# Read-back of the first products of a SwiGLU layer, moved behind one-element copies, with its stores on GpSimd's queue

## The chip, the cores and the metric

The kernel runs on one core of a Trainium2 chip. The metric is device time in microseconds (us): the median of the runs of one program. PE is TensorE's matmuls, PEld its weight loads, DVE is VectorE, ACT is ScalarE, POOL is GpSimd, and SPq is the queue of the sync engine, which issues most of the DMAs. L1422 is line 1422 of the kernel.

## The reference

One step of an encoder layer for two groups of tokens that share weights: 1024 prompt tokens and 64 sample tokens, 1088 together, 1024 channels, fp32. The layer has stick-breaking attention beside an mLSTM, a merge by gates and an output projection; then the feed-forward part, which is where the change lies:

```python
u2 = _rmsnorm(x, norm2_g) * (1 + sc2) + sh2
x = x + g2 * ((jax.nn.silu(u2 @ w_ff_gate) * (u2 @ w_ff_up)) @ w_ff_down)
```

`w_ff_gate` and `w_ff_up` are 1024 by 2816, `w_ff_down` is 2816 by 1024. At the end comes one more RMSNorm.

## The kernel before, in words

Matmuls run in fp32r with each operand split in a high and a low part, three matmuls for one product. Gate, up and down products use a Strassen-like scheme with seven products for eight (numbered p, in the order 1, 6, 5, 7, 2, 3, 4), over sums and differences of weight blocks and of quarters of the tokens.

The 2816 feed-forward channels are 22 blocks of 128. One run of `gate_up(i, h, ...)` makes block i for half h of the tokens (544 of them): seven products of 12 matmuls, each evacuated from PSUM by `evac(p)`. At p = 6 VectorE writes the tile `u2`, which the later products of the same run read (the tag has one buffer). The product tile `hst`, two quarters of 272 tokens, is stored to `h_d` in memory by the sync queue at L1375.

The jobs are, in order: blocks 0 to 9 for half 0 alone (job k = 0 to 9, `NF` is 10); blocks 10 to 21 for both halves (jobs 10 to 21); blocks 0 to 9 for half 1. For blocks 0 to 9 the weight sums come ready-made from memory (`wsum_d`), seven loads a job by L1310. From block 10 on the raw gate and up weights are loaded (L1298), and GpSimd makes the sums S (L1324, L1325, L1331, L1334). ScalarE casts a weight to its high part (L47), VectorE makes the low part by a difference (L56). The raw weights have three buffers and one smaller one, the split weights seven, one for each product.

The down product reads `h_d` and, in `tb_d` and `tc_d`, sums and differences of the products of neighbouring blocks. For most of them `pair_sums` makes these on VectorE when the products are there (L1404 to L1414). For half 0 of blocks 0 to 9 they are made by `first_sums`, a generator with five steps j: it loads the products of blocks 2j and 2j + 1 from `h_d` into the two halves of the one tile `tj` (L1422, L1423), and at its next call makes four sums on GpSimd (L1425 to L1428) and stores both halves (L1429, L1430). It is called at p = 6 in each half of jobs 10 to 21, ten calls in all: `step(early_sums)` in `hook`. While jobs 0 to 9 run, `todo` makes the modulated input of the second half, on VectorE and ScalarE.

The program text is not the order of issue: a scheduler that keeps a time line of its own puts each instruction on its engine's queue when its operands, its buffer and its engine are free by that time line. On the chip each engine and each queue then works strictly in that order, and waits for the semaphores of what its instruction depends on. The downward products start about 1583 us into the profiled span.

Of the kernel before, what the change touches and what calls it, by code (L numbers as in the profile page):

```python
# [26 lines left out]
HT = T // 2  # L27
# [8 lines left out]
def trunk(ctx, tc, a, o, dbg=None, stop=None):  # L36
    nc = tc.nc
# [160 lines left out]
    cur = {}  # L198
# [1079 lines left out]
    tb_d = dram.tile([FP, P, T], F32, name="tb_d")  # L1278
    tc_d = dram.tile([FP, P, T], F32, name="tc_d")

    def tq(tag, name):
        return gp.tile([P, QT], F32, tag=tag, name=name, bufs=1)
# [62 lines left out]
    def gate_up(i, h, ws, after, job):  # L1345

        hst = product_tile(i, h, job)
        h0, h1 = hst[:, :QT], hst[:, QT:]
        ba, bb, bc, bd = (gb.tile([P, 512], F32, tag="g", name=f"ps_{x}{i}_{h}", bufs=8)[:, :QT] for x in ("ga", "gb", "gc", "gd"))
        bank_of = {1: ba, 2: ba, 6: bb, 5: bc, 3: bc, 7: bd, 4: bd}  # L1350
        t = {}

        def evac(p):
            if p == 1:
                t["p1"] = tq("p1", f"p1_{i}_{h}")
                nc.scalar.copy(t["p1"], ba)
            elif p == 6:
                t["u2"] = tq("u2", f"u2_{i}_{h}")
                nc.vector.tensor_sub(t["u2"], t["p1"], bb)
            elif p == 5:  # L1360
                nc.vector.tensor_add(h1, bc, t["u2"])  # L1361
            elif p == 7:
                nc.vector.tensor_add(h1, bd, h1)  # L1363
            elif p == 2:
                t["g0"] = tq("g0", f"g0_{i}_{h}")
                nc.scalar.activation(t["g0"], ba, AF.Silu)  # L1366
            elif p == 3:
                t["g1"] = tq("g1", f"g1_{i}_{h}")
                nc.vector.tensor_add(t["g1"], bc, t["u2"])
                nc.scalar.activation(t["g1"], t["g1"], AF.Silu)  # L1370
                nc.vector.scalar_tensor_tensor(h1, h1, -1.0, t["g1"], ALU.mult, ALU.mult)
            else:
                nc.vector.tensor_add(h0, bd, t["u2"])  # L1373
                nc.vector.scalar_tensor_tensor(h0, h0, -1.0, t["g0"], ALU.mult, ALU.mult)  # L1374
                nc.sync.dma_start(h_d[i][:, HT * h : HT * (h + 1)], hst)  # L1375

        for p in order:
            w, (oh, ol), ps = ws[p], ops[h, p], bank_of[p]
            for j in range(4):
                for k, (a, b) in enumerate(((0, oh), (0, ol), (1, oh))):  # L1380
                    nc.tensor.matmul(ps, w[:, a, j, :], b[j // 2][:, j % 2, :], start=p in (1, 6, 5, 7) and j == 0 and k == 0,  # L1381
                                     stop=j == 3 and k == 2, skip_group_check=True)
            evac(p)
            if job >= NF and i % 2:
                pair_sums(i, h, hst, p)
            after(p)
# [5 lines left out]
    def product_tile(i, h, job):  # L1392

        if job < NF or i % 2:
            return gp.tile([P, HT], F32, tag="hst", name=f"hst{i}_{h}", bufs=2)
        held[h] = npl.tile([P, HT], F32, tag="rr" if (h if job < FFB else i // 2 % 2) else "t2", name=f"hst{i}_{h}", bufs=1)
        return held[h]

    def pair_sums(i, h, hst, p):

        b, r = held[h], slice(HT * h, HT * (h + 1))
        b0, b1, c0, c1 = b[:, :QT], b[:, QT:], hst[:, :QT], hst[:, QT:]
        if p == 7:
            nc.vector.tensor_sub(b0, b0, b1)  # L1404
        elif p == 3:
            nc.vector.tensor_sub(b1, c1, b1)
            nc.sync.dma_start(tb_d[i // 2][:, r], b)
            held["t2"] = npl.tile([P, QT], F32, tag="sq2", name=f"T2_{i}_{h}", bufs=4)
            nc.vector.tensor_add(held["t2"], c1, b0)
            nc.sync.dma_start(tc_d[i // 2][:, HT * h + QT : HT * (h + 1)], held["t2"])  # L1410
        elif p == 4:
            t4 = npl.tile([P, QT], F32, tag="sq2", name=f"T4_{i}_{h}", bufs=4)
            nc.vector.tensor_sub(t4, held["t2"], c0)
            nc.sync.dma_start(tc_d[i // 2][:, HT * h : HT * h + QT], t4)  # L1414

    def first_sums():

        t = up.tile([P, T], F32, tag="u", name="tj")
        b, c = t[:, :HT], t[:, HT:]
        b0, b1, c0, c1 = b[:, :QT], b[:, QT:], c[:, :QT], c[:, QT:]  # L1420
        for j in range(NF // 2):
            nc.sync.dma_start(b, h_d[2 * j][:, :HT])  # L1422
            nc.sync.dma_start(c, h_d[2 * j + 1][:, :HT])  # L1423
            yield
            nc.gpsimd.tensor_sub(b0, b0, b1)  # L1425
            nc.gpsimd.tensor_sub(b1, c1, b1)
            nc.gpsimd.tensor_add(c1, c1, b0)
            nc.gpsimd.tensor_sub(c0, c1, c0)  # L1428
            nc.sync.dma_start(tb_d[j][:, :HT], b)  # L1429
            nc.sync.dma_start(tc_d[j][:, :HT], c)  # L1430
            yield

    dn = {}
# [29 lines left out]
    def gbank(name):  # L1463
        return gb.tile([P, 512], F32, tag="g", name=name, bufs=8)

    early_sums = first_sums()
    todo = chain([rstd_rows(1, sqs, rows2[1], gbank), modulate2(1, 0, rows2[1]), modulate2(1, 1, rows2[1])])
    for k, (i, halves) in enumerate(jobs):
# [254 lines left out]
```

## Time and profile before

| | |
|---|---|
| median of 3 runs | 1810.19 us (1808.59 to 1813.41) |
| profiled execution | 1818.29 us |
| its span, first to last instruction | 1816.6 us |
| mean granted TensorE clock | 0.98 |
| busy share PE, PEld, DVE, ACT, POOL | 95%, 92%, 58%, 40%, 31% |
| DMA: sync engine's queue, GpSimd's queue (share of 16 engines) | 50.2%, 10.2% |
| loads L1422 of `tj` | 5, first at 1115.5, last at 1203.0 us |
| stores L1430 of `tj` | 5, first at 1127.0, last at 1217.9 us |

Matmuls are pipelined, so a busy TensorE is not TensorE at its peak. A row of a list of work reads: start, length, engine, line, operation, out<-in, shapes, count; a bracket at the end holds how long the engine stood idle just before, and what ended that. A row of waits reads: who <- whom: total us, times, longest. Such a releaser is inferred from semaphores, the last to come.

### The profile page before, as it was taken

How to read it: one execution, taken by the hardware profiler on the slowest of the kernel's cores; microseconds unless marked ns; L12 is line 12 of the kernel's file. 1: busy time of each engine (PE TensorE's matmuls, PEld its weight loads, DVE VectorE, ACT ScalarE, POOL GpSimd, SP SyncE). 2: the span in 40 equal slices, each digit the busy share in tenths (PEclk: the TensorE clock that was granted, in tenths of full speed). 3: DMA queues.
4: the chain of work that ended last, by engine and by line, in shares of the span. 5: the costliest groups of instructions: out<-in, count | busy, mean ns of one | idle time of the engine just before them, and what ended most of it. 6: DMA issues, size and time to landing. Idle time of an engine off the chain costs nothing. (4 is left out here: it accounts for less than half of the span.)

```text
span 1816.6 us, 32764 instructions
## 1 busy us (share of the span) xinstructions
PE 1733.0 (95%) x12670; PEld 1667.9 (92%) x12670; DVE 1050.2 (58%) x2014; ACT 734.3 (40%) x1500; POOL 562.4 (31%) x497
## 2 busy tenths in 40 slices
PE   5899999999999999989898999999999999999998
PEld 4699999899988988878898998999999999999998
DVE  6633415152356858686553389655555577657965
ACT  5332333324234535353422457433222354443444
POOL 2434534445442232315876241142222100000000
PEclk9999999999999999999998999999999999999999
DMA  9426666664485565686576346753333488899852
GB/s 266 119 67 204 144 199 139 191 165 142 128 210 139 138 160 128 155 256 190 164 221 185 98 136 184 211 168 107 108 104 97 140 243 234 269 339 353 293 159 99
DMA packets 360174, 320.26 MB, mean 176 GB/s; under 512 B 16726, under 2 KB 327506, under 8 KB 360018
## 3 DMA queue, kind: packets, MB, share of 16 engines
q1 hardware_dynamic: 346514, 273.56, 50.2%
q0 software_dynamic: 13504, 44.60, 10.2%
q8 instruction: 100, 1.64, 0.4%
q14 instruction: 56, 0.46, 0.1%
HBM read 241.01 MB, written 98.09 MB: 187 GB/s over the span
## 5 line engine op out<-in xcount | busy, mean ns | idle before, releaser
L1605 PE MATMUL ps_d<-o,wh_d 128*128 128x272 f32 x1232 | 230.8, 288 | 0.0
L1605 PEld LDWEIGHTS ps_d<-o,wh_d 128*128 128x128 f32 x1232 | 192.9, 188 | 0.0
L1605 PE MATMUL ps_d<-o,wl_d 128*128 128x272 f32 x616 | 176.7, 288 | 0.0
L1605 PEld LDWEIGHTS ps_d<-o,wl_d 128*128 128x128 f32 x616 | 115.8, 189 | 0.0
L396 DVE TENSOR_TENSOR_SCAN re<-re 128x128 f32<-128x128 f32 (+3 forms) x64 | 106.5, 1665 | 14.7 <-ACT re L392 14.3
L47 ACT CAST w<-wr 128x512 fp32r<-128x512 f32 x140 | 85.0, 619 | 69.7 <-PE ps_gd L1381 15.6
L56 DVE TENSOR_TENSOR w<-wr,w 128x512 fp32r<-128x512 f32 x140 | 96.5, 702 | 25.9 <-ACT w L47 23.8
L1589 POOL DMA_DIRECT2D dsum_d<-wr_d x12 | 6.5, 543 | 237.7 <-DVE wr_d L1587 229.0
L1381 PE MATMUL ps_ga<-b1h,w 128*128 128x272 f32 x352 | 74.8, 290 | 4.0 <-ACT g L1366 2.9
L1381 PE MATMUL ps_gd<-b7h,w 128*128 128x272 f32 x352 | 74.5, 291 | 3.7 <-DVE hst L1373 3.6
L392 ACT ACTIVATE re<-z 128x512 f32<-128x512 f32 (+2 forms) x96 | 47.5, 495 | 74.9 <-DVE z L388 57.3
L1381 PE MATMUL ps_gb<-b6h,w 128*128 128x272 f32 x352 | 75.4, 293 | 2.2 <-ACT w L47 1.2
L1381 PE MATMUL ps_gc<-b3h,w 128*128 128x272 f32 x352 | 74.1, 290 | 1.9 <-DVE hst L1361 1.9
L1381 PE MATMUL ps_gd<-b4h,w 128*128 128x272 f32 x352 | 75.1, 293 | 0.6 <-DVE hst L1363 0.5
L1381 PE MATMUL ps_gc<-b5h,w 128*128 128x272 f32 x352 | 75.0, 293 | 0.1
L1381 PE MATMUL ps_ga<-b2h,w 128*128 128x272 f32 x352 | 73.9, 289 | 0.0
L47 ACT CAST o<-hr 128x544 fp32r<-128x544 f32 x77 | 48.8, 645 | 50.6 <-DMA hr<-h_d 26.0
L76 PE MATMUL ps_ga<-uh,wh_ga 128*128 128x384 f32 (+1 forms) x192 | 65.2, 340 | 3.3 <-ACT gt_ga L825 3.2
L47 ACT CAST wh_d<-wr_d 128x1024 fp32r<-128x1024 f32 (+1 forms) x42 | 41.1, 979 | 67.1 <-PE ps_d L1605 32.5
L56 DVE TENSOR_TENSOR o<-hr,o 128x544 fp32r<-128x544 f32 x77 | 53.8, 720 | 21.7 <-ACT o L47 21.5
L76 PE MATMUL ps_gb<-uh,wh_gb 128*128 128x384 f32 (+1 forms) x192 | 64.9, 338 | 0.0
L77 PE MATMUL ps_ga<-ul,wh_ga 128*128 128x384 f32 (+1 forms) x192 | 64.5, 336 | 0.0
(547 smaller groups left out, 5897.9 us busy)
## 6 DMA issues: line engine op xcount, KB each, us to landing
wada<-in_w_ada SPq DMA_DIRECT2D x48, 512.0 KB
wr<-wsum_d SPq DMA_DIRECT2D x80, 256.0 KB
wr_d<-in_w_ff_down SPq DMA_DIRECT2D x34, 512.0 KB
h_d<-hst SPq DMA_DIRECT2D x44, 272.0 KB
wr<-in_w_ff_gate SPq DMA_DIRECT2D x40, 256.0 KB
hr<-h_d SPq DMA_DIRECT2D x33, 272.0 KB
wsum_d<-in_w_ff_up POOLq DMA_DIRECT2D x6, 1282.0 KB, 7.7
wsum_d<-in_w_ff_gate POOLq DMA_DIRECT2D x6, 1282.0 KB, 7.7
```

What stands on the lines that cost most here:

```text
L47: nc.scalar.copy(out, in_)
L56: nc.vector.tensor_sub(out, in_, h.bitcast(F32))
L76: nc.tensor.matmul(ps, wh, xh, start=first, stop=False)
L77: nc.tensor.matmul(ps, wh, xl, start=False, stop=False)
L392: nc.scalar.activation(rest[:, c0 : c0 + w], ps, AF.Sigmoid, scale=-scale)
L396: nc.vector.tensor_tensor_scan(r, r, r, 1.0, ALU.mult, ALU.bypass)
L1381: nc.tensor.matmul(ps, w[:, a, j, :], b[j // 2][:, j % 2, :], start=p in (1, 6, 5, 7) and j == 0 and k == 0, stop=j == 3 and k == 2, skip_ ...
L1589: nc.gpsimd.dma_start(dsum_d[p][mp, ks[0] // 4][:, : P * n], flat)
L1605: nc.tensor.matmul(ps, a[:, j, mi, :], b[:, h], start=p not in (2, 4) and k == ks[0] and i == 0, stop=k == ks[-1] and i == 2, skip_group_c ...
```

## The change

Three edits. `evac` keeps the newest `u2` in the dictionary `cur`. `first_sums` writes, ahead of each pair of loads, one element of that `u2` into one element of each half of `tj`, on VectorE; the loads overwrite the whole halves, so what is computed stays the same, and each load depends on a `u2` of the run of `gate_up` in whose hook it is called. The stores of the sums are issued by GpSimd and no more by the sync engine.

```diff
             elif p == 6:
                 t["u2"] = tq("u2", f"u2_{i}_{h}")
                 nc.vector.tensor_sub(t["u2"], t["p1"], bb)
+                cur["u2"] = t["u2"]
...
         for j in range(NF // 2):
+
+            for x in (b, c):
+                nc.vector.tensor_copy(x[0:1, 0:1], cur["u2"][0:1, 0:1])
             nc.sync.dma_start(b, h_d[2 * j][:, :HT])
             nc.sync.dma_start(c, h_d[2 * j + 1][:, :HT])
             yield
...
-            nc.sync.dma_start(tb_d[j][:, :HT], b)
-            nc.sync.dma_start(tc_d[j][:, :HT], c)
+            nc.gpsimd.dma_start(tb_d[j][:, :HT], b)
+            nc.gpsimd.dma_start(tc_d[j][:, :HT], c)
             yield
```

## The prediction

> **What bounds the kernel now.** I read the page first, then the stretches of the gate and up stage, then TensorE's own waits, then the sync queue's, and last the chain across the place of the change. In the stretches the first number is the length, and after it stand the busy times of TensorE (PE), its weight loads, VectorE, ScalarE and GpSimd, the granted clock and the DMA share.
>
> ```profile
> span 1816.6 us, 32764 instructions
> PE 1733.0 (95%) x12670; PEld 1667.9 (92%) x12670; DVE 1050.2 (58%) x2014; ACT 734.3 (40%) x1500; POOL 562.4 (31%) x497
> ...
> 1100.00:1150.00 50.00, 44.54 (x335) 43.63 (x334) 43.14 (x77) 29.03 (x56) 5.62 (x5) 0.97 0.72 205
> 1150.00:1200.00 50.00, 48.05 (x380) 47.63 (x379) 35.09 (x64) 21.91 (x43) 13.11 (x13) 1.00 0.78 225
> 1200.00:1250.00 50.00, 46.50 (x349) 45.40 (x348) 27.74 (x56) 15.62 (x31) 17.02 (x15) 0.97 0.38 121
> 1250.00:1300.00 50.00, 50.00 (x400) 50.00 (x399) 27.13 (x57) 13.90 (x28) 13.93 (x11) 1.00 0.38 119
> ```
>
> TensorE is the bound, so only its idle time and its slow clock can be won. From 1100 to 1250 us, the single-half jobs 0 to 9 and the passage to job 10, it misses 5.46 + 1.95 + 3.50 = 10.9 us; from 1250 on it misses nothing. The gaps one by one (idle time before the row in brackets, with what ended it):
>
> ```profile
> 1133.24 0.39 PE L1381 MATMUL ps_ga<-b1h,w 128*128 128x272 f32 x1 [2.87 <-ACT g L1366]
> 1145.80 0.36 PE L1381 MATMUL ps_gd<-b7h,w 128*128 128x272 f32 x1 [1.73 <-DVE hst L1373]
> ...
> 1158.94 0.36 PE L1381 MATMUL ps_gd<-b7h,w 128*128 128x272 f32 x1 [1.88 <-DVE hst L1373]
> ...
> 1202.60 0.39 PE L1381 MATMUL ps_gb<-b6h,w 128*128 128x272 f32 x1 [1.18 <-ACT w L47]
> ...
> 1222.23 0.39 PE L1381 MATMUL ps_gc<-b3h,w 128*128 128x272 f32 x1 [1.91 <-DVE hst L1361]
> ```
>
> The read-back of the first products sits in just this stretch. It is written for jobs 10 to 14, yet its loads are issued while jobs 0 to 9 still store those products, and the sync queue, which issues in order, stands behind them. Its waits from 1098 to 1222 us (total, times, longest):
>
> ```profile
> SPq L1423 <- DMA h_d<-hst: 16.1, 5, 5.6
> SPq L1429 <- POOL tj L1426: 15.2, 5, 3.9
> SPq L1422 <- DMA h_d<-hst: 11.5, 4, 4.1
> ...
> SPq L1430 <- POOL tj L1428: 5.9, 4, 1.7
> ```
>
> That is 48.7 us in a queue that also carries seven weight loads per job. L1422 and L1423 wait until a product just computed has landed in memory, L1429 and L1430 until GpSimd has summed. What was queued behind:
>
> ```profile
> 1124.53 0.33 SPq L1429 DMA_DIRECT2D tb_d<-tj  x1
> 1124.91 0.43 SPq L1310 DMA_DIRECT2D wr<-in_w_ff_gate  x1
> ...
> 1137.22 0.33 SPq L1422 DMA_DIRECT2D tj<-h_d  x1
> ...
> 1138.08 4.55 SPq L1310 DMA_DIRECT2D wr<-wsum_d  x3
> ```
>
> And who on ScalarE and VectorE waited for those loads:
>
> ```profile
> 1128.23 0.62 ACT L47 CAST w<-wr 128x512 fp32r<-128x512 f32 x1 [1.46 <-DMA wr<-in_w_ff_gate]
> ...
> 1143.95 0.62 ACT L47 CAST w<-wr 128x512 fp32r<-128x512 f32 x1 [1.95 <-DMA wr<-wsum_d]
> ```
>
> At the passage to job 10 the chain of waits itself runs through the read-back (start, length, what):
>
> ```profile
> 1196.03 0.78 POOL tj L1426
> ...
> 1199.24 1.29 POOL S L1324
> 1200.61 1.29 POOL S L1325
> 1201.93 0.63 ACT w L47
> ...
> 1212.35 2.68 DMA tj<-h_d
> ...
> 1217.93 0.32 SPq L1430
> 1218.31 2.38 DMA h_d<-hst
> 1220.78 0.10 DVE hst L1404
> ```
>
> **The change part by part: what goes.** The ten one-element copies make each load of tj wait for the u2 of the job in whose hook it is written, so no load can be issued before job 10's first u2; its row stands at gap 4. The whole read-back moves behind it, into the first 100 us of the jobs of two halves. I cost each gap:
>
> 1. 1145.80: its chain goes back through the cast at 1143.95 to the sum load issued at 1138.08, behind L1422, which went out at 1137.22 after up to 4.1 us of waiting. A load 4 us sooner removes the cast's 1.95 us of waiting, and so the gap: 1.73 us.
>
> 2. 1158.94: partly the same delay handed on, partly VectorE slowed while GpSimd sums j = 1. Two weight differences that take 1.28 us with GpSimd idle took 2.38 us there:
>
> ```profile
> 1099.29 1.28 DVE L56 TENSOR_TENSOR w<-wr,w 128x512 fp32r<-128x512 f32 x2
> ...
> 1155.15 2.38 DVE L56 TENSOR_TENSOR w<-wr,w 128x512 fp32r<-128x512 f32 x2
> ```
>
> I take half of the gap, 0.94 us; the rest may be the wait for a weight buffer, which stays.
>
> 3. 1202.60: GpSimd's sums of the read-back (L1426 from 1196.03, until S L1324 could start at 1199.24) hold up the weight sums that the cast at 1201.93 needs. They were 3.2 us; the gap of 1.18 us goes.
>
> 4. 1222.23: VectorE stands at L1404 until the product store issued at 1218.31 has landed, 2.38 us later. That store's data was there 4.7 us before its issue (1213.17 + 0.44 = 1213.6), and the queue stood at L1423, L1429 and L1430:
>
> ```profile
> 1207.48 0.42 DVE L1359 TENSOR_TENSOR u<-p,ps_gb 128x272 f32<-128x272 f32 x1
> ...
> 1213.17 0.44 DVE L1374 SCALAR_TENSOR_TENSOR hst<-hst,g 128x272 f32<-128x272 f32 x1
> ```
>
> Issued at 1213.6 it lands at 1216.0, before VectorE gets to L1404. The gap of 1.91 us goes.
>
> 5. 1133.24: the weight load at 1124.91 stood behind L1429, and the cast at 1128.23 waited 1.46 us for it. But VectorE is busy without a break there (43.14 of 50 us in that stretch, with the modulation of the second half in it), so of 2.87 us I take 1.46.
>
> 6. The clock. After the gaps of 2.87 and 1.91 us the granted clock falls:
>
> ```profile
> 1130.00:1140.00 10.00, 7.13 (x44) 6.91 (x44) 5.87 (x12) 3.82 (x9) 0.01 (x1) 0.83 0.61 184
> ...
> 1220.00:1230.00 10.00, 8.09 (x52) 7.87 (x51) 6.42 (x13) 2.86 (x6) 2.21 (x2) 0.83 0.23 67
> ```
>
> 0.83 over 10 us is 1.7 us of work lost each time. The second dip I count as won (1.7 us), since its gap goes whole; the first I leave, since part of its gap stays.
>
> By the Trainium skill, "TensorE: Matmul & The Clock Gate", What's actually happening, the clock halves after an idle window of about 3.4 us; both gaps are shorter, and by that rule the dips would not be theirs and the sum would be 1.7 us less. The trace disagrees in part: dips follow the gaps of 2.87 and 1.91 us, while the stretch from 1150 to 1200 us, with the gap of 1.88 us in it, keeps 1.00.
>
> Sum of the gains: 1.73 + 0.94 + 1.18 + 1.91 + 1.46 + 1.7 = 8.9 us. With everything in the list (the rest of 2 and 5 and the first dip, 0.94 + 1.41 + 1.7) it would be 13.0 us; with 3 and 4 and their dip alone 4.8 us.
>
> **What is added, and where it comes to lie.** Ten copies on VectorE. The nearest small row is the copy of one element per partition, 144 ns; ten are 1.4 us in about 100 us in which VectorE is busy 27.13 of 50 and TensorE misses nothing, so I take zero; beyond that cover it would be 1.4 us at most. Ten stores issued by GpSimd instead of the sync queue: 0.54 us each by the nearest such row, 5.4 us, in a stretch in which GpSimd is busy 13.93 of 50; zero too. The sums take 20.19 us for all five steps, 4.0 us each.
>
> ```profile
> L781 DVE COPY ncol<-C 128x1 f32<-128x1 f32 x8 | 1.2, 144 | 0.0
> ...
> L435 POOL DMA_DIRECT2D qs<-qk_d x16: 509/542/619, 498.7 to 787.3; - x16
> ...
> DMA to landing us min/median/max: 3.7/5.8/13.1
> ...
> 1110.00:1222.00 112.00, 20.19 (x20) 0.98 0.70 205
> ...
> 1230.03 0.44 DVE L1359 TENSOR_TENSOR u<-p,ps_gb 128x272 f32<-128x272 f32 x1 [1.28 <-PE ps_gb L1381]
> ```
>
> The new waits are three. The sync queue waits at L1422 and L1423 for the copies; behind them stand the wide weight loads of the next job and the product stores, of which each job of two halves needs only half as many a block as before, and the sync queue no longer stands for a landing or for GpSimd. The copies of step j + 1 overwrite what the stores of step j read, so VectorE, in order, stands at them until those stores have landed; behind them are the evacuations of TensorE's banks and the weight differences. And on GpSimd the sums come between the weight sums of the next job (S, L1324 to L1334). The cycle: from one step's u2 at 1207.48 to the next one's at 1230.03 are 22.5 us. A load of tj lands 2.68 us after issue; two, one behind the other, I estimate at 4. Sums 4.0, two issues on GpSimd 1.1, landing 5.8 in the median of the nearest GpSimd DMAs of the same 272 KB: 15 us, with 7 to spare. So VectorE does not wait; the price if it does is below. What is late next in jobs 0 to 9, with the read-back gone, is the weight buffer: a load is issued only when the difference that reads the buffer is done. The stretch from 1150 to 1200 us, 48.05 of 50 busy even with the read-back in it, says that this cycle nearly keeps up.
>
> **The rivals.**
>
> Half the gain (the read-back was not what was late). For it: VectorE's 43.14 of 50 us from 1100 to 1150, and casts that wait for weight buffers anyway. Gaps 1, 2 and 5 would then come back from VectorE and the buffers, 3 and 4 with their dip go: -4.8 us, 1805.4 us. Against it: gap 1 is traced row by row to L1422.
>
> No change: the waits move with the loads, and gaps as wide open in jobs 10 to 14, each late store or load costing about what it cost before. Against it: from 1250 to 1300 us TensorE misses nothing and the DMA share is 0.38, where it was 0.72 to 0.78. Time: 1810.
>
> Slower: the copies stand on VectorE for GpSimd's stores. It decides when a store lands more than 22.5 - 4 - 4.0 - 1.1 = 13.4 us after its issue; the slowest of the nearest rows is 13.1. At four steps (the first has nothing to wait for), each with a stall as at 1220.78, which cost 1.91 us and a dip of 1.7, that is 14.4 us against 8.9 won: +5.5, 1815.7 us. Against it: the rows with 13.1 us are from a stage where GpSimd issues many such DMAs one behind the other, here two per 22.5 us.
>
> The Trainium skill, "SBUF — State Buffer", Who interferes with whom, speaks for that rival: a DMA issued by GpSimd has its descriptors written through a port pair that VectorE shares, so it can starve there, while one issued by the sync queue cannot. No run here shows yet how long these stores take beside VectorE's work of jobs 10 to 14.
>
> That the change does not do what it says would mean that the loads still run early; the copies read u2 of jobs that come later, so I give that nothing.
>
> **How the numbers follow.** The sum is made against the profiled execution, 1818.29 us (span 1816.6 and 1.7 around it), which lies 8.1 us above the median shown; 8.9 us less there is 1809.4, and against the median 1810.19 it is 1801.3. Chances: the forecast, 5.5 to 13.5 us won, 0.58; half the gain, 2 to 5.5 us, 0.22; no change, 0.10; slower by over 5.4 us 0.05 and by less 0.05. About 0.3%, 5.4 us, is what a measurement of this kernel can tell from no change. So faster by more than that 0.62 (the forecast and a little of the half gain), within it 0.32, slower by more 0.06. The range reaches from the full list (13.0 and one more dip of 1.7, 14.7 us: 1795.5) to just short of no change, 1808.5; it leaves out no change and slower, 0.20 in all. The forecast's own range is 1797 to 1805.
>
> **What would show it.** In the changed kernel's trace the first load of tj should be issued after job 10's first u2; the sync queue's waits for landings of h_d and for GpSimd should be gone; the gaps 1145.80, 1202.60 and 1222.23 should be missing, and one near 1133 should stay, shorter; VectorE should have no wait at the copies for the stores. Wrong would make it: waits on VectorE ended by landings of tb_d and tc_d, new gaps between 1210 and 1310 us, or a stretch 1100 to 1200 us that still misses 7 us with no read-back in it.

## The result, and the profile after

| kernel | median us (runs) | kernel before beside it (runs) | ratio, 95% interval |
|---|---|---|---|
| changed | 1794.76 (4) | 1809.39 (4) | 0.9920 [0.9899, 0.9941] |
| changed, again | 1797.10 (6) | 1808.31 (23) | 0.9944 [0.9922, 0.9965] |

The change makes the kernel faster by 14.6 us in the first comparison and by 11.2 us in the second, about 12 us in all. The forecast was 8.9 us won and 1801.3 us; the first median lies 0.7 us under the low end of the range, 1795.5, and the second inside it.

In the changed kernel and those made from it the lines behind `evac` are numbered one higher than before, and in `first_sums` L1425 are the copies, L1426 and L1427 the loads, L1429 to L1432 the sums, L1433 and L1434 the stores.

The profiled execution took 1791.73 us, 26.6 us less than that of before. Not all of that is the change. This row of each kernel is the stretch from the start of the span to the first gate matmul, which does the same work in both (columns: stretch, length, busy time of TensorE, weight loads, VectorE, ScalarE, GpSimd, granted clock, DMA share, GB/s). First before, then changed:

```profile
0.00:1077.73 1077.73, 1010.89 (x6964) 951.24 (x6965) 558.09 (x1093) 418.95 (x937) 474.40 (x417) 0.97 0.60 164
```

```profile
0.00:1065.44 1065.44, 1001.77 (x6964) 943.63 (x6965) 559.66 (x1093) 418.89 (x937) 472.83 (x417) 0.98 0.60 166
```

12.3 us of the difference lie there. In the profiles of the other kernels below this stretch took 1063.4 to 1071.8 us, whatever they did behind it: the 1077.73 us of the profile that the prediction worked from are its worst. The two repeats of before are next, with 1071.1 and 1071.8 us; why, no run shows. So I compare stage by stage: from the last gate and up matmul of block 0 to the last of the twelfth run of `gate_up`, which takes in jobs 1 to 9 and both halves of job 10. Before, in the profile shown and in the two repeats (`r1_before`, `r3_before`), one fence each:

```profile
1093.98:1226.60 132.62, 121.91 (x928) 119.70 (x926) 98.24 (x175) 65.05 (x125) 30.69 (x28) 0.98 0.65 189
```

```profile
1087.94:1217.41 129.47, 122.19 (x927) 119.90 (x926) 98.47 (x174) 64.31 (x123) 30.53 (x28) 0.97 0.66 193
```

```profile
1087.38:1219.04 131.66, 120.58 (x928) 118.35 (x927) 98.20 (x174) 64.26 (x123) 30.84 (x28) 0.99 0.65 190
```

Changed, with the next ten runs of `gate_up` in a second row, and then the repeat (`r2_after`):

```profile
1081.72:1200.75 119.03, 116.94 (x927) 116.50 (x926) 95.24 (x177) 65.41 (x125) 15.67 (x14) 1.00 0.59 173
1200.75:1306.22 105.47, 105.47 (x841) 105.47 (x840) 64.23 (x134) 32.82 (x66) 42.58 (x44) 1.00 0.45 146
```

```profile
1084.80:1204.30 119.50, 117.23 (x927) 116.59 (x926) 95.06 (x177) 65.23 (x125) 15.72 (x14) 1.00 0.59 172
```

The stage takes 131.25 us in the mean of three profiles before. With the tie it takes 119.38 in the mean of these two and of the tie alone (119.62, below). That is 11.9 us, about the whole gain by the medians. TensorE's idle time, length less busy, goes from 10.71, 7.28 and 11.08 us to 2.09, 2.27 and 2.52: 7.4 us in the means. The granted clock goes from 0.98, 0.97 and 0.99 to 1.00 throughout. The clock's records in the traces say why: in the stage the three profiles of before have two, two and one dips of 3.41 us at 0.50, those with the tie none. A dip loses 1.7 us of work, so this is 2.8 us in the mean. One of them, in `r1_before`:

```profile
1128.20:1131.60 3.40, 3.40 (x17) 3.40 (x16) 1.62 (x4) 0.00 (x0) 0.00 (x0) 0.50 0.48 147
```

The second row of the changed kernel is where the read-back now lies: GpSimd works 42.58 us there and TensorE misses nothing. What is left in the stage is, in TensorE's waits from 1085 to 1310 us (who <- whom: total us, times, longest), nearly one gap:

```profile
PE ps_ga L1382 <- ACT g L1367: 1.9, 1, 1.9
PE ps_gd L1382 <- DVE hst L1374: 0.2, 1, 0.2
```

Of the seven gaps that the list of waits gives for the stage in the profile the prediction worked from, it is the one at 1133.24, 1.0 us shorter. The sync queue's largest wait in total from 1085 to 1195 us, against the list of before:

```profile
SPq L1310 <- DVE w L56: 18.7, 12, 3.4
```

In its list up to 1310 us no wait is left for a landing of `h_d` or for a sum of `tj`. The queue stands at weight buffers (w, L56) instead: it is ahead of the work. And the read-back at its new place, instructions on the tile `tj`; the landings are those of the ten stores (count, shortest, median and longest ns, first and last start):

```profile
L1425 DVE COPY tj<-u x10: 130/142/143, 1184.7 to 1268.0; 1x1 f32<-1x1 f32 x10
L1426 SPq DMA_DIRECT2D tj<-h_d x5: 319/347/831, 1185.1 to 1268.0; - x5
...
L1433 POOL DMA_DIRECT2D tb_d<-tj x5: 549/552/615, 1192.4 to 1277.2; - x5
...
L1434 POOL DMA_DIRECT2D tc_d<-tj x5: 547/547/547, 1194.1 to 1278.9; - x5
...
DMA to landing us min/median/max: 2.3/2.4/4.5
```

### The profile page after: what moved, and what is told of

Same layout as the page of the kernel before. It is cut to its first block, busy times and chain, and to the rows that moved or that the text cites. A ratio compares the mean times of both kernels' runs of the same rounds, so it can differ in the third digit from the quotient of the medians.

```text
span 1790.0 us, 32786 instructions
## 1 busy us (share of the span) xinstructions
PE 1718.5 (96%) x12670; PEld 1656.9 (93%) x12670; DVE 1052.6 (59%) x2024; ACT 735.2 (41%) x1500; POOL 563.0 (31%) x507
## 5 line engine op out<-in xcount | busy, mean ns | idle before, releaser
L56 DVE TENSOR_TENSOR w<-wr,w 128x512 fp32r<-128x512 f32 x140 | 94.9, 691 | 21.4 <-ACT w L47 17.6
L47 ACT CAST wh_d<-wr_d 128x1024 fp32r<-128x1024 f32 (+1 forms) x42 | 41.2, 981 | 66.6 <-PE ps_d L1609 26.6
L56 DVE TENSOR_TENSOR o<-hr,o 128x544 fp32r<-128x544 f32 x77 | 53.9, 723 | 21.0 <-ACT o L47 20.6
L56 DVE TENSOR_TENSOR al<-ps_a,ah 128x512 fp32r<-128x512 f32 (+1 forms) x80 | 49.3, 631 | 25.7 <-ACT ah L47 25.3
```

The costliest lines, as they stand in the source:

```text
L47: nc.scalar.copy(out, in_)
L56: nc.vector.tensor_sub(out, in_, h.bitcast(F32))
```

## The experiments

The question was which of four things had cost the time: the sync queue standing at the read-back, GpSimd's sums, the transfers beside the weight loads, or the stores on the sync queue alone. Each row shown is the stage defined above, from that kernel's profile. The two repeats come first.

**Before and changed again.**

> The kernel before, once more, for its profile. The two half-clock windows of 3.4 us in its gate and up stage: if they belong to the gaps of 2.87 and 1.91 us, the same gaps come again (within 0.5 us each) and a dip after each of them or most of them; if they are chance, the gaps come again without the dips, and the stage from the end of block 0 to the end of the twelfth run is some 3 us shorter than 132.6 us.

> The changed kernel once more, beside more runs of the kernel before. If the surplus over the predicted 8.9 us is in the stage (14.4 us between the two profiles), the ratio stays near 0.992 (13 to 16 us). If a part of it is chance of the few runs, the ratio comes out at 0.993 to 0.995 (9 to 12 us), nearer to the two kernels with half of the change undone or replaced.

> The kernel before a third time, for its profile: from the end of block 0 to the end of the twelfth run it took 132.6 and 129.5 us in the first two. If its gaps are set by the program, it stays within 129 to 133 us, with a gap of 2.8 to 2.9 us at the second modulation; the gaps after it vary.

Their rows stand above. Before has gaps near 39, 64 and 128 us into the stage in each profile (1133.24, 1158.94 and 1222.23 in the first). The others differ: at the places of 1145.80 and 1202.60 `r1_before` has 0.22 us at most, and `r3_before` has one of 2.17 us where the others have less than 0.1. A dip does not follow every gap either: in `r1_before` one of 1.92 us has one, in `r3_before` those of 1.90 to 2.17 us have one in four. So the stage takes 129.47 to 132.62 us. The changed kernel and the tie alone stay within 0.6 us of each other. The one execution of `r1_before` took 1807.91 us and that of `r3_before` 1810.21.

**The stores alone.**

```diff
-            nc.sync.dma_start(tb_d[j][:, :HT], b)
-            nc.sync.dma_start(tc_d[j][:, :HT], c)
+            nc.gpsimd.dma_start(tb_d[j][:, :HT], b)
+            nc.gpsimd.dma_start(tc_d[j][:, :HT], c)
```

> The kernel before with the ten stores alone moved to GpSimd's queue; the loads stay untied. Theory (the gaps come from the sync queue standing at the read-back's own waits): 27.6 of its 48.7 us of waiting, those at the two loads, stay, 21.1 go; the read-back stays in jobs 0 to 9. 3 to 5 us won, with gaps left near 1145, 1202 and 1222 us. Rival (the stores' waits for GpSimd's sums were what held the weight loads): 10 us or more won, and little left between 1090 and 1230 us.

1802.86 us (12 runs) against 1808.97 (17), 0.9967 [0.9953, 0.9981]. The stage, and then the sync queue's waits of the read-back from 1085 to 1215 us:

```profile
1083.80:1210.10 126.30, 118.64 (x926) 116.73 (x925) 99.69 (x174) 64.80 (x124) 34.58 (x38) 1.00 0.68 198
```

```profile
SPq L1423 <- DMA h_d<-hst: 17.0, 5, 4.4
SPq L1422 <- DMA h_d<-hst: 8.5, 4, 3.0
...
SPq L1422 <- DMA tb_d<-tj: 1.9, 1, 1.9
```

The waits for GpSimd are gone, those for the landing of the products stay. About half of the gain comes with the first kind: 6.1 us by the medians, a little more than expected, and 5.0 in the stage.

**The loads alone.** Only L1422 and L1423 issued by GpSimd, nothing else changed.

```diff
-            nc.sync.dma_start(b, h_d[2 * j][:, :HT])
-            nc.sync.dma_start(c, h_d[2 * j + 1][:, :HT])
+            nc.gpsimd.dma_start(b, h_d[2 * j][:, :HT])
+            nc.gpsimd.dma_start(c, h_d[2 * j + 1][:, :HT])
```

> The kernel before with the ten loads alone moved to GpSimd's queue, untied; the stores stay on the sync queue. The counterpart of the kernel with the stores alone moved, which won 6 us, and a part of the one with both on GpSimd, which won 8.5. Theory (what counts is how long the sync queue stands in jobs 0 to 9, whoever it stands for): the waits for landings of h_d go, but the stores then wait there for loads and sums, as in the kernel without the sums, so 2 to 6 us are won. Rival (the loads' waits for fresh products are the greater part by themselves): 8 us or more.

1802.97 us (11 runs) against 1808.99 (22), 0.9967 [0.9956, 0.9977]; the stage, and the sync queue's largest wait in the same window:

```profile
1086.53:1210.68 124.15, 118.93 (x927) 116.89 (x926) 96.44 (x174) 64.24 (x123) 36.25 (x38) 1.00 0.69 202
```

```profile
SPq L1429 <- POOL tj L1426: 26.1, 5, 8.3
```

The other half by itself wins as much: 6.0 us by the medians, 7.1 in the stage. GpSimd now waits for the product to land, and the stores, still on the sync queue, wait for GpSimd longer than before (8.3 against 3.9 us at most).

**Loads and stores on GpSimd, untied.** Both diffs together: the read-back stays in jobs 0 to 9, with its sums and its transfers, and only its queue is another.

> The kernel before with loads and stores of the read-back issued by GpSimd, untied: the transfers and the sums stay in jobs 0 to 9, only the sync queue no longer stands behind them. Theory: most of what the sync queue's waits cost comes back, 8 to 11 us won; the gap near 1202 us stays, since GpSimd's sums still stand ahead of the weight sums of job 10, and VectorE's differences are still slowed beside the sums. Rival (the read-back's transfers share the DMA engines with the weight loads, and that makes these late): 0 to 3 us won.

1799.97 us (6 runs) against 1808.97, 0.9953 [0.9935, 0.9971]. The stage, GpSimd's work at the passage to job 10, and TensorE's gap there:

```profile
1080.04:1201.31 121.27, 117.82 (x926) 116.57 (x925) 102.89 (x175) 64.85 (x124) 40.06 (x48) 1.00 0.69 207
```

```profile
1177.17 0.79 POOL L1428 TENSOR_TENSOR tj<-tj 128x272 f32<-128x272 f32 x1
1177.91 1.28 POOL L1324 TENSOR_TENSOR S<-wr_u 128x512 f32<-128x512 f32 x1
```

```profile
1180.25 0.36 PE L1381 MATMUL ps_gd<-b4h,w 128*128 128x272 f32 x1 [0.27 <-DVE hst L1363]
```

Here the DMA share is as high as before (0.69), GpSimd is busier (40.06 us, with its twenty issues) and VectorE is slowed (102.89 us busy, against 98.2 to 98.5 before). Yet 10.0 of the 11.9 us are won. The sums sit ahead of S at the passage as they did before, and the only gap of TensorE there is 0.27 us, where I had expected the gap near 1202 to stay. So neither the sums nor the transfers were most of what the place cost; the queue was.

One rival is left by the edit itself: it takes the transfers, too, off the queue that carries the weights, so that these might land sooner after their issue. They do not. By the semaphore updates in the traces, the 52 loads of L1310 in the stage take 4.01, 3.88 and 4.18 us from issue to landing in the mean of each profile before, 4.05 here, 3.66 in the changed kernel and 3.67 without a read-back. What came sooner is the issue.

**No sums.** The four sums of each step left out, all else as before.

```diff
-            nc.gpsimd.tensor_sub(b0, b0, b1)
-            nc.gpsimd.tensor_sub(b1, c1, b1)
-            nc.gpsimd.tensor_add(c1, c1, b0)
-            nc.gpsimd.tensor_sub(c0, c1, c0)
```

> The kernel before with GpSimd's four sums of the read-back left out (the loads and stores stay untied on the sync queue, so the down product reads unsummed products there). It tells what the sums themselves cost: VectorE slowed beside them, the weight sums of job 10 behind them, and the sync queue's 21.1 us of waits for them, in whose place the stores now wait for the loads to land. Theory: 3 to 6 us won; the gap near 1202 us goes, the waits at the loads stay and with them gaps near 1145 us. Rival (the sums were the greater part): 9 us or more won.

1810.19 us (12 runs) against 1808.31 (23), 1.0007 [0.9993, 1.0021]: nothing won, where I expected 3 to 6 us. The stage, the sync queue's waits from 1085 to 1215 us (L1425 and L1426 are the stores here), and casts that stood idle ahead of job 10:

```profile
1086.08:1216.44 130.36, 120.54 (x928) 118.36 (x926) 94.53 (x175) 64.26 (x124) 10.94 (x8) 0.99 0.66 192
```

```profile
SPq L1422 <- DMA h_d<-hst: 18.9, 4, 5.5
SPq L1423 <- DMA h_d<-hst: 16.1, 5, 5.4
SPq L1426 <- DMA tj<-h_d: 12.3, 5, 3.6
SPq L1425 <- DMA tj<-h_d: 6.4, 5, 1.9
```

```profile
1170.05 0.62 ACT L47 CAST w<-wr 128x512 fp32r<-128x512 f32 x1 [3.46 <-DMA wr<-in_w_ff_gate]
...
1186.76 0.62 ACT L47 CAST w<-wr_g 128x512 fp32r<-128x512 f32 x1 [4.75 <-DMA wr_g<-in_w_ff_gate]
```

GpSimd works 10.94 us instead of 30.7, and VectorE 94.53 instead of 98.2. Still the queue stands 53.7 us at the read-back: without sums the stores wait for the landing of the loads. Casts still wait for late weights, and TensorE is idle for 9.8 us, against 9.7 in the mean before.

**The tie alone.** The changed kernel, copies and `cur` with it, with the stores given back to the sync queue.

```diff
-            nc.gpsimd.dma_start(tb_d[j][:, :HT], b)
-            nc.gpsimd.dma_start(tc_d[j][:, :HT], c)
+            nc.sync.dma_start(tb_d[j][:, :HT], b)
+            nc.sync.dma_start(tc_d[j][:, :HT], c)
```

> The changed kernel with its ten stores back on the sync queue; the copies stay. Theory: as fast as the changed kernel within 3 us (12 to 15 us under before), since in jobs 10 to 14 the sync queue has few weight loads to hold up. Rival (the stores' queue matters there as well): 4 us or more slower than the changed kernel, with TensorE gaps between 1180 and 1290 us.

1798.68 us (6 runs) against 1808.97, 0.9949 [0.9933, 0.9965].

```profile
1085.82:1205.44 119.62, 117.10 (x928) 116.50 (x926) 94.07 (x176) 64.38 (x123) 15.10 (x12) 1.00 0.59 172
1205.44:1311.00 105.56, 105.56 (x841) 105.51 (x840) 64.44 (x134) 33.49 (x67) 38.31 (x37) 1.00 0.45 146
```

The tie gives the whole gain in the stage. Behind it the sync queue now stands for loads and sums of `tj` (its waits up to 1310 us):

```profile
SPq L1433 <- DMA tj<-h_d: 17.9, 5, 4.7
SPq L1433 <- POOL tj L1430: 8.9, 5, 1.8
SPq L1434 <- POOL tj L1432: 7.0, 5, 1.5
```

That is 33.8 us, more than in either half-way kernel, and TensorE, busy in all of the 105.56 us of the second row, does not feel it: the queue has room there that it does not have in jobs 0 to 9. Once the loads are tied, the stores' queue makes no difference that the runs can tell.

**No read-back.** `first_sums` issues nothing, and the operands are taken from `h_d`, so that what is computed is not the same: the ceiling of any move.

```diff
-        for j in range(NF // 2):
+        for j in range(0):
...
+        if k < NF // 2 and p not in (1, 2, 3):
+            src = h_d[2 * k + p % 2]
```

> The kernel before without the read-back: no loads of tj, no sums, no stores for half 0 of blocks 0 to 9; the down operands that would read those sums read the products themselves from h_d, so half of the down product of these blocks is another number, and its work is the same. Theory: 14 to 16 us won, no more than 2 us beyond the changed kernel, with a gap of 1 to 2 us left where VectorE modulates. Rival (the moved read-back still costs something in jobs 10 to 14, or its loads delay others there): 18 us or more won.

1794.73 us (6 runs) against 1808.97, 0.9928 [0.9908, 0.9948], not to be told from the changed kernel.

```profile
1084.01:1204.76 120.75, 118.36 (x928) 117.95 (x926) 94.38 (x175) 65.23 (x125) 11.29 (x8) 0.99 0.56 161
1204.76:1310.59 105.83, 105.81 (x841) 105.59 (x840) 60.84 (x126) 32.89 (x66) 25.39 (x20) 1.00 0.33 103
```

The moved read-back costs nothing where it now is: 105.47 us with it, 105.83 without.

**One step for each call.** The `yield` between loads and sums removed from the changed kernel: twice the pace, each copy close behind the last stores.

```diff
             nc.sync.dma_start(c, h_d[2 * j + 1][:, :HT])
-            yield
             nc.gpsimd.tensor_sub(b0, b0, b1)
```

> The changed kernel with no pause between loads and sums: one step of the read-back per run of gate_up, so the copies of one step come about 10.6 us after those of the step before. In the changed kernel a step takes 11.4 us from the first load's issue to the landing of the last store (1185.1 to 1196.4 us), so here copies are ready to wait for stores. Rival of the prediction (VectorE stands at the copies, each such stall makes a TensorE gap of some 2 us and a dip): 6 to 14 us slower than the changed kernel. Theory (a stall of 1 to 2 us is covered by the banks in flight, and TensorE loses nothing): within 2 us of the changed kernel, with no gap between 1180 and 1290 us.

1803.82 us (12 runs) against 1808.31, 0.9976 [0.9963, 0.9990]: 6.7 us slower than the changed kernel beside it (1797.10). My own theory, covered and within 2 us, fell. The loss is in the ten runs behind the passage, with these gaps:

```profile
1199.16:1311.44 112.28, 107.47 (x841) 107.03 (x839) 68.10 (x132) 33.21 (x67) 42.88 (x44) 0.98 0.41 132
```

```profile
1210.05 0.39 PE L1382 MATMUL ps_gd<-b4h,w 128*128 128x272 f32 x1 [1.79 <-DVE hst L1364]
...
1233.02 0.53 PE L1382 MATMUL ps_gc<-b3h,w 128*128 128x272 f32 x1 [3.01 <-DVE hst L1362]
```

VectorE also waited at the copies for stores, 2.6 us in two places. Whether that was the price the next run asked.

**The same with the copies on GpSimd.** So VectorE no longer stands at them.

```diff
-                nc.vector.tensor_copy(x[0:1, 0:1], cur["u2"][0:1, 0:1])
+                nc.gpsimd.tensor_copy(x[0:1, 0:1], cur["u2"][0:1, 0:1])
```

> The kernel with one step of the read-back per run of gate_up, with its copies on GpSimd instead of VectorE. With them on VectorE the stage from the twelfth to the 22nd run took 112.3 us against 105.5. If the loss comes from VectorE standing at the copies: 4 us or more of it come back, and no TensorE gap stands behind a copy. If it comes from the sums falling beside VectorE's own sums of pairs: 2 us or less come back.

1804.20 us (12 runs) against 1808.99, 0.9968 [0.9954, 0.9981]: nothing came back. The ten runs, and the longest gap in them:

```profile
1203.95:1315.91 111.96, 107.21 (x841) 106.76 (x839) 66.98 (x126) 33.00 (x67) 44.51 (x50) 0.98 0.42 133
```

```profile
1237.68 0.59 PE L1382 MATMUL ps_gc<-b3h,w 128*128 128x272 f32 x1 [3.53 <-DVE hst L1362]
```

This is what VectorE, and then GpSimd, did ahead of it; the last fence is a wait of the sync queue in these runs:

```profile
1220.91 0.44 DVE L1414 TENSOR_TENSOR T<-T,hst 128x272 f32<-128x272 f32 x1
...
1231.99 1.53 DVE L1410 TENSOR_TENSOR T<-hst,hst 128x272 f32<-128x272 f32 x1
1233.44 1.51 DVE L1375 SCALAR_TENSOR_TENSOR hst<-hst,g 128x272 f32<-128x272 f32 x1
1234.99 1.76 DVE L1414 TENSOR_TENSOR T<-T,hst 128x272 f32<-128x272 f32 x1
```

```profile
1231.87 1.36 POOL L1324 TENSOR_TENSOR S<-wr_u 128x512 f32<-128x512 f32 x1 [0.71 <-DMA wr_u<-in_w_ff_up]
1233.18 1.48 POOL L1331 TENSOR_TENSOR S<-wr_g,wr_u 128x512 f32<-128x512 f32 x1
...
1235.16 1.27 POOL L1325 TENSOR_TENSOR S<-S,wr_g 128x512 f32<-128x512 f32 x1
```

```profile
SPq L1298 <- POOL S L1334: 6.1, 2, 3.7
```

Three operations of VectorE with both inputs in SBUF take 1.51 to 1.76 us while GpSimd sums, against 0.43 to 0.44 alone. The excess, 1.10 + 1.08 + 1.32 = 3.5 us, is as long as the gap, and the evacuation L1362 that ends it stands behind them; ahead of the gap of 3.01 us in the kernel above the same three take 1.52 to 1.76 us. How GpSimd's weight sums came to lie there, the traces show too: the weight sum L1334 stands on GpSimd behind a sum of `tj` that waited for its load, the sync queue waits for that weight sum before it loads the next raw weights, a wait that the changed kernel does not have in these runs, and so the next weight sums come later. That this makes up the loss is read from the traces; no run takes these sums away at this pace.

**VectorE relieved in the gap that is left.** In the changed kernel the sums of the second half's modulation go to GpSimd, which is idle in jobs 1 to 9.

```diff
+        v = nc.gpsimd if h else nc.vector
...
-        nc.vector.tensor_sub(b11, b11, b12)
+        v.tensor_sub(b11, b11, b12)
...
-        nc.vector.tensor_add(t2, b22, b11)
+        v.tensor_add(t2, b22, b11)
...
-        nc.vector.tensor_sub(b11, t2, b21)
+        v.tensor_sub(b11, t2, b21)
...
-        nc.vector.tensor_sub(b12, b22, b12)
+        v.tensor_sub(b12, b22, b12)
```

> The changed kernel with the four sums and differences of the second half's modulated input made by GpSimd, which now stands idle in jobs 0 to 9. They are in the place of the one gap left, 1.8 us near 1118 us, where VectorE is busy without a break. If VectorE's load is its cause and GpSimd is quick enough: the gap goes, 1 to 2 us faster than the changed kernel, within what can be told. Rival (two engines reading the same memory hold each other up, and GpSimd is slower at the same sum): the split inputs come later, the gap grows, 1 to 5 us slower.

1794.43 us (6 runs) against 1808.99, 0.9922 [0.9898, 0.9945]: not to be told from the changed kernel (0.9920 and 0.9944). The stage and TensorE's waits from 1085 to 1310 us:

```profile
1085.66:1206.52 120.86, 117.40 (x928) 116.77 (x927) 96.16 (x169) 65.17 (x125) 29.49 (x22) 1.00 0.58 170
```

```profile
PE ps_gd L1383 <- ACT w L47: 1.9, 2, 1.3
PE ps_ga L1383 <- ACT g L1368: 1.6, 1, 1.6
```

The gap shrinks by 0.3 us, and two others come, behind casts. What makes the last gap stays open; that VectorE's modulation sums make it was not borne out. No version tried clearly beats the changed kernel.

**What they say together.** Five kernels have the read-back in jobs 0 to 9. The sync queue's standing for its landings and sums, in total, against the length of the stage: 53.7 us and 130.36 (no sums), 48.7 and 132.62 (before), 32.4 (26.1 + 3.4 + 2.9) and 124.15 (loads moved), 27.4 (17.0 + 8.5 + 1.9) and 126.30 (stores moved), none and 121.27 (both moved). But for two swaps of neighbours they fall in the same order; GpSimd's busy time (10.94, 30.69, 36.25, 34.58, 40.06) and the DMA share (0.66, 0.65, 0.69, 0.68, 0.69) go the other way or nowhere. What is left between 121.27 and 119.4, about 1.9 us, is what these profiles leave for sums and transfers. By the medians, 9.0 us won against 11.2 and 14.6, it may be 2 to 6 us.

## Why the prediction came out as it did

The mechanism was right, and its bound on the place too: about all that was won was won in the stage named, most of it by weight loads that no longer queue behind the read-back, and nothing was paid behind it. The size was too small, and one attribution does not hold as it was put. By its own steps:

- *Gap 1145.80* (1.73 taken): gone in every profile with the tie. Right, though `r1_before` does not have it either.
- *Gap 1158.94* (0.94 taken, "partly VectorE slowed while GpSimd sums"): gone whole, and in the untied kernel, whose sums stay, too. So the half that I withheld, 0.94 us, came too.
- *Gap 1202.60* (1.18 taken, GpSimd's sums named): gone, but the sums alone do not make it. They stand ahead of S in `r1_before` as well, where 0.22 us is the most that is missed at this place, and in the untied kernel, where 0.27 us is missed just ahead of it. Without the sums, with the queue as it was, 0.49 us is left at this place, but TensorE misses 2.15 us just ahead of it, and casts at the passage waited up to 4.75 us for weights. The sums were last in the chain; the lateness was mostly the loads'.
- *Gap 1222.23* (1.91 taken): gone. Right.
- *Gap 1133.24* (1.46 taken): 1.0 us came, 1.87 is left, and what holds it is open.
- *Idle time as a sum*: the five terms add up to 7.22 us; the means over profiles give 7.4. That they agree so well is partly luck: in the profile that I worked from it went from 10.71 to 2.09, by 8.6 us, in `r1_before` there were only 7.28 to begin with, and the terms withheld and the smaller gaps that I left out came in part.
- *The clock* (1.7 us, "the first I leave, since part of its gap stays"): this is the step that failed. The dips of before are two, two and one in the stage, 2.8 us in the mean, and none came in any profile with the tie at the pace of the change, although a gap of 1.8 to 1.9 us stays. That the stay of a gap keeps its dip was my reason, and it did not hold: about 1.1 us too little, and 1.7 against the profile I worked from, whose two dips both went. The kernel without a read-back, with the same gap, has one dip, so that none came is chance in part.
- *A term that was missing*, put at nothing: a gap costs TensorE more than its bracket says. The rows around gap 1145.80 of before show it, the last matmul ahead of it and the first two behind:

```profile
1143.78 0.29 PE L1381 MATMUL ps_gc<-b5h,w 128*128 128x272 f32 x1
1145.80 0.36 PE L1381 MATMUL ps_gd<-b7h,w 128*128 128x272 f32 x1 [1.73 <-DVE hst L1373]
1146.00 0.29 PE L1381 MATMUL ps_gd<-b7l,w 128*128 128x272 f32 x1
```

In step, 841 matmuls in 105.47 us of the changed kernel's second row are 0.125 us each; across the gap it is 2.02 us from start to start, and 0.20 for the next. The loss is 2.02 + 0.20 - 2 * 0.125 = 1.97 us where the bracket says 1.73, because the bracket starts at a modelled end, 0.29 us after the start. That is 0.24 us for this gap, and 0.24 to 0.27 by the same working for the others of 0.2 us and more in these profiles. The three profiles of before have eight, nine and nine gaps in the stage, down to 0.07 us; those with the tie have two or three. Six fewer make about 1.5 us, and with 7.4 and 2.8 that is 11.7 of the 11.9 us. By the Trainium skill, "Perfetto Trace Analysis", Per-engine timelines, the end of a matmul in a profile is an estimate; the rows here agree.

So 7.2 and 1.7 were forecast where 7.4, 2.8 and about 1.5 came. The low end, the full list with one more dip, held nothing for that last term: it stands 14.7 us below 1810.19. The first four runs came out 14.6 us below their own 1809.39, the next six 11.2 below theirs. That the first median lies under the range owes to a kernel before that ran 0.8 us faster beside it, and, as the second comparison makes likely, to the chance of few runs. By the means of the stage the forecast was 3 us short.

The rivals: *half the gain* fell, since all five gaps answered. *No change* fell: from the passage on TensorE misses nothing with the read-back there. *Slower, the copies stand on VectorE for GpSimd's stores* fell at the pace of the change: stores landed 2.4 us after issue in the median (I took 5.8, from rows of a stage in which many such DMAs are queued), so a step was over 11.4 us after its first load (1185.1 to 1194.1 + 2.4 = 1196.5) where I had worked out 15, against a period of 22.5. At twice the pace VectorE does stand there, 2.6 us, but that was not what the pace cost. By the Trainium skill, "SBUF — State Buffer", Who interferes with whom, VectorE can starve a DMA that GpSimd issues; these ten stores landed in 2.3 to 4.5 us, and VectorE had no wait for them. By its "DMA: Bandwidth & Descriptors", Anatomy of one DMA — SWDGE (gpsimd) path, such a DMA takes about 2.0 us and its bytes over 436 GB/s, 2.6 us as an estimate for 272 KB: the median of the trace agrees, and my row was the wrong one.

## What to carry to other kernels

Look at what the queue that carries your loads stands at, not only at what it moves: a load that needs a result just computed makes every weight behind it late, and 48.7 us of standing cost about 10 us of a bound engine although the bytes and the arithmetic cost little; 33.8 us in a stage whose loads had room cost nothing. Either issue such a transfer from a queue on which nothing urgent waits, or make it depend on something later, so that it is ready when its turn comes; when the second was done here, the first added nothing that the runs can tell. When you size gaps of TensorE, take start to start less the steady step, add the dips of the clock that a repeat shows too, and do not read the engine that released last as the cause without a run that takes it away.

## What the runs showed that I had not expected

- Three VectorE operations of 128x272 with two inputs in SBUF took 1.51 to 1.76 us beside GpSimd's sums, 0.43 to 0.44 without. The Trainium skill, "SBUF — State Buffer", Who interferes with whom, says that such an operation contends with a GpSimd instruction that reads SBUF; the trace agrees. At twice the pace three of them in a row stood ahead of gaps of 3.0 and 3.5 us.
- The Trainium skill, "DMA: Bandwidth & Descriptors", Issuing engines are not separate DMA queues, says that issuing from several engines saves only the time of issue. Here twenty issues of about 0.33 us, 6.6 us of an engine that does not bound, moved to another engine and won 10.0 us in the stage with the same transfers. What was saved is the waiting at the head of the queue, and by the measurement that can be the larger part.
- Dips of the clock came after gaps of 1.9 to 2.9 us in some profiles of one program and not in others: two, two and one in the same stage, each 3.41 us at 0.50.
